# An encoder layer whose turned inputs come from the host, with a new opening

## The chip, the cores and the metric

The kernel runs on one core of a Trainium2 chip. The metric is the device time of one execution in microseconds (us), the median of several runs. Five engines work beside each other, each through its own instructions in a fixed order: TensorE (PE, matmuls and transposes; PEld is its loading of weights), VectorE (DVE), ScalarE (ACT), GpSimd (POOL) and SyncE (SP), which here issues nearly all DMA transfers. Across engines, semaphores hold an instruction back until what it reads is there and what it overwrites has been read.

## The reference

One layer over 2048 tokens of 1024 features, all in 32-bit floats:

```python
u = _rms_norm(h, norm_mix_g[l])
proj = u @ w_in[l]                                   # 1024 x 3600
hy = _short_conv_centred(proj[..., :HY_COLS], ...)   # 1536 columns
spec = _hyena_filter_spectrum(L, ...)                # from the weights alone
y_hy = _group_rms_norm(_hyena(hy, spec, hy_skip[l]), ...)
qk = jax.nn.silu(_short_conv_centred(proj[..., HY_COLS:off], ...))
y_ml = _group_rms_norm(_mlstm_bidirectional(qk, v, o, gates), ...)
h = h + concat(y_hy, y_ml) @ w_out[l]
h = h + _cross_attention(_rms_norm(h), _rms_norm(mem), xa_wq, xa_wk, xa_wv, xa_wo)
h = h + squared_relu(_rms_norm(h) @ ff_w1) @ ff_w2
out = _rms_norm(h, final_norm_g)
```

`_rms_norm(x, g)` is x / sqrt(mean(x*x over the 1024 features) + 1e-6) * g. The Hyena part convolves by FFT twice, gating after each; `mem` has 256 tokens.

## The kernel before, in words

A matmul contracts over the partition axis, so activations are needed with features on partitions ("turned") while `x` lies in memory with tokens as rows. Precision comes from splitting each 32-bit operand into a rounded high part and the remainder (`split`, L299: a copy on ACT, then a subtraction on DVE) and summing three products (`mm3`, lines 295 to 297).

**Opening and projection.** Half of x (1024 tokens) at a time lies turned, normalised and split in `xh` and `xl`. `prep` (L425) makes it tile by tile of 128 tokens: load rows (L401), square and sum on ACT (L409), a reciprocal root in eleven small DVE instructions (`rsqrt`, L144), scaling (L414), eight PE transposes of 128x128 (L420), a split into `xh` and `xl`. It is run for the first half, then the second, the first again, and for `mem`; `pop` advances it by a tile between matmul groups. `sweep` (L512) takes 256 columns of w_in at a time and runs four groups (two token blocks of 512 by two column blocks of 128) of 24 matmuls each, then the width-3 convolution, transposes of its result (`sweep_out`, L576) and stores; `natural` (L605) does the v, o and gate columns in 272- or 256-column matmuls.

**Filters and Hyena.** `filters` (L158) makes the filter spectrum: a small network (L208, L212), windows (L253, L238), writes to a scratch tensor `fs`, then 32 blocks that read it back, multiply (L284) and write `hd`. `hyena` (L638) runs two orders, each with a first transform (L720), 16 blocks that read `zs` and `hd` and write `zg` (L734, L702), and a last one (L753). `weave` takes steps of two generators in a fixed ratio: filters beside the first 1024 columns of w_in for both halves, Hyena beside the rest. All tensors between stages go through memory, so that a stage's reads wait for the writes before it.

**Later stages.** `memproj` (L458) projects mem and folds Wq and Wo into it; Wq is needed turned and `turned` (L331) does that with four PE transposes (L341) for each of 16 loads. `attention` (L1061) goes over four chunks of 512 tokens; its `residual` (L1131) loads rows of x, transposes them on PE (`turn`, L1106) and copies them into `acc`. Then comes the MLP.

A planner orders every engine's instructions before the run: program order is its input, but it moves instructions past each other where data allow. `keep_in_program_order` holds an instruction to its written place on its engine. A load from SP that must wait for its buffer holds all loads and stores behind it on SP.

```python
            p.prep_x(0, True)
            p.pop(4)
            s = chain(p.sweep(range(4), 0, True, lambda: p.prep_x(1)), p.sweep(range(4), 1, False))
            next(s)
            next(s)
            weave(p.filters(), s, 230, 200)
```

Of the kernel before, what the change touches and what calls it, by code (L numbers as in the profile page):

```python
# [19 lines left out]
D = 1024  # L20
# [77 lines left out]
class Prog:  # L98
    def __init__(self, ctx, tc, a):
        self.tc, self.nc, self.a = tc, tc.nc, a  # L100
        nc = self.nc
        self.ctx = ctx
        self.dr = ctx.enter_context(tc.tile_pool(name="dr", bufs=1, space=DRAM))
        self.s = {}
        cp = self.cp = ctx.enter_context(tc.tile_pool(name="cp", bufs=1))
        ident = cp.tile([128, 128], F32, name="ident")
        nc.gpsimd.memset(ident, 1.0)
        nc.gpsimd.affine_select(ident, ident, pattern=[[-1, 128]], compare_op=ALU.is_equal, fill=0.0,
                                base=0, channel_multiplier=1)
# [7 lines left out]
        self.prepq = None  # L117
        self.rbp = cp.tile([128, 16], F32, name="rbp")
        self.ps = ctx.enter_context(tc.tile_pool(name="ps", bufs=1, space=PSUM))
# [38 lines left out]
    def filters(self):  # L158
# [3 lines left out]
        with tc.tile_pool(name="f_sb", bufs=1, side="right") as sb:  # L162
# [56 lines left out]
            def windows(j2):  # L219
                if j2 == 8:  # L220
                    return None
                w = ta(), ta()
                for r in range(2):
                    nc.sync.dma_start(out=w[r], in_=wv[r, :, 2 * j2:2 * j2 + 2])
                return w
# [39 lines left out]
            def blocks(o, i):  # L265
                p, k = divmod(2 * i, 16)
                dm = sb.tile([128, 2, 128], F32, tag="dm", name="dm", bufs=3)
                nc.sync.dma_start(out=dm, in_=a["c_dm"][:, 2 * i:2 * i + 2])
# [30 lines left out]
    def split(self, hi, lo, src):  # L299
        self.nc.scalar.copy(hi, src)  # L300
        self.nc.vector.tensor_tensor(lo, src, hi.bitcast(F32), ALU.subtract)  # L301
# [10 lines left out]
    def weights(self, pool, w, n, kc=4, bufs=2, nbufs=2):  # L312
# [12 lines left out]
        for k0 in range(0, kt, kc):  # L325
            nat = pool.tile([128, kc, n], F32, tag="wn", name="wn", bufs=nbufs)
            nc.sync.dma_start(out=nat, in_=w[128 * k0:128 * (k0 + kc), :].rearrange("(k p) c -> p k c", p=128))
            self.split(hi[:, k0:k0 + kc], lo[:, k0:k0 + kc], nat)
        return hi, lo

    def turned(self, pool, w):  # L331
        nc = self.nc
        hi = pool.tile([128, 2, 1024], F32R, tag="wh", name="wh", bufs=2)
        lo = pool.tile([128, 2, 1024], F32R, tag="wl", name="wl", bufs=2)
        for i in range(4):
            nat = pool.tile([128, 2, 256], F32, tag="wn", name="wn", bufs=3)
            nc.sync.dma_start(out=nat, in_=w[256 * i:256 * i + 256, :].rearrange("(k p) c -> p k c", p=128))
            pt = self.mm()
            for m in range(2):
                for k in range(2):  # L340
                    nc.tensor.transpose(pt[:, 256 * m + 128 * k:256 * m + 128 * k + 128],  # L341
                                        nat[:, k, 128 * m:128 * m + 128], self.ident)
            ds = slice(256 * i, 256 * i + 256)
            self.split(hi[:, :, ds], lo[:, :, ds], pt.rearrange("p (m c) -> p m c", m=2))
        return hi, lo

    def stream(self, pool, items, **kw):
        nxt = None
        for i in range(len(items) + 1):
            cur = nxt  # L350
            if i < len(items):
                w, n = items[i]
                nxt = self.turned(pool, w) if n is None else self.weights(pool, w, n, **kw)
            if cur is not None:
                yield cur
# [3 lines left out]
    def inproj_open(self, es):  # L359
# [9 lines left out]
        self.g_mix = self.bcast(sb, a["norm_mix_g"], D, "g_mix")  # L369
        self.turned_to = lambda h: (self.xh[:, 4 * h:4 * h + 4], self.xl[:, 4 * h:4 * h + 4])  # L370
# [8 lines left out]
        nc.gpsimd.dma_start(out=self.cb[:, 12:20], in_=a["ml_conv_b"].rearrange("o (k p) -> p (o k)", p=128))  # L379
        self.gb = sb.tile([128, 16], F32, name="gb")  # L380
# [7 lines left out]
        second = [(a["xa_wq"][0][:, h], None) for h in hs] + [(a["xa_wo"][0][h, :], 1024) for h in hs]  # L388
# [4 lines left out]
        self.wst = self.stream(sb, items, kc=2, nbufs=3)  # L393

    def prep_load(self, src, first, i):
        sb = self.isb
        if first and i % 3:
            xn = sb.tile([128, 1042], F32, tag=("P", "cv")[i % 3 - 1], name="xn", bufs=2)[:, 0:D]
        else:
            xn = sb.tile([128, D], F32, tag="xn", name="xn", bufs=2)  # L400
        self.nc.sync.dma_start(out=xn, in_=src)  # L401
        return xn

    def prep_norm(self, xn, gain):
        nc, sb = self.nc, self.isb
        ss = sb.tile([128, 2], F32, tag="ss", name="ss", bufs=2)
        for h in range(2):
            junk = sb.tile([128, 512], F32, tag="st", name="junk", bufs=3)
            nc.scalar.activation(junk, xn[:, 512 * h:512 * h + 512], AF.Square, accum_out=ss[:, h:h + 1])  # L409
        ms = sb.tile([128, 1], F32, tag="ms", name="ms", bufs=2)  # L410
        nc.vector.tensor_tensor(ms, ss[:, 0:1], ss[:, 1:2], ALU.add)
        nc.vector.tensor_scalar(ms, ms, 1.0 / D, EPS, ALU.mult, ALU.add)
        rv = self.rsqrt(sb, ms, "xr")
        nc.vector.scalar_tensor_tensor(xn, xn, rv, gain, ALU.mult, ALU.mult)  # L414

    def prep_turn(self, xn, t):
        for h in range(2):
            p = self.mm().rearrange("p (k t) -> p k t", k=4)
            for k in range(4):
                self.nc.tensor.transpose(p[:, k], xn[:, 512 * h + 128 * k:512 * h + 128 * k + 128], self.ident)  # L420
            hi, lo = self.turned_to(h)
            ts = slice(128 * t, 128 * t + 128)
            self.split(hi[:, :, ts], lo[:, :, ts], p)

    def prep(self, src, gain, first=False):  # L425
        n = src.shape[0] // 128
        ahead = 5 if first else 1
        q = []
        for i in range(n + ahead):
            if i < n:  # L430
                xn = self.prep_load(src[128 * i:128 * i + 128, :], first, i)
                q.append(xn)
            if i >= ahead:
                xn = q.pop(0)
                self.prep_norm(xn, gain)
                self.prep_turn(xn, i - ahead)
                yield
# [6 lines left out]
    def prep_x(self, hf, first=False):  # L444
        self.prepq = self.prep(self.a["x"][1024 * hf:1024 * hf + 1024, :], self.g_mix, first)

    def mem_open(self):
        self.g_mem = self.isb.tile([128, D], F32, tag="g_mix", name="gm", bufs=1)
        self.nc.gpsimd.dma_start(out=self.g_mem, in_=self.a["norm_mem_g"].broadcast_to([128, D]))

    def prep_mem(self):
        sb = self.isb
        gm = self.g_mem
        self.memt = [[sb.tile([128, 4, 256], F32R, tag=tag, name="mt", bufs=2) for tag in ("P", "cv")] for h in range(2)]
        self.turned_to = lambda h: self.memt[h]
        self.prepq = self.prep(self.a["mem"], gm)
# [55 lines left out]
    def sweep(self, cols, hf, first, after=None):  # L512
        nc, a, sb = self.nc, self.a, self.isb
        xh, xl, cw, cb, carry = self.xh, self.xl, self.cw, self.cb, self.carry
        for c2 in cols:
# [8 lines left out]
            for c in range(2):  # L524
                for m in range(2):
# [5 lines left out]
                    for k in range(8):  # L531
                        self.mm3(p, wh[:, k, ms], wl[:, k, ms], xh[:, k, cs], xl[:, k, cs], k == 0, k == 7)
                    if c == 0:
# [527 lines left out]
    def attention(self, es):  # L1061
# [65 lines left out]
        stats = None  # L1127
        for c in range(4):
            acc = T.tile([128, 8, 512], F32, tag="acc", name="acc")

            def residual(h):  # L1131
                q = [rows(a["x"], 512 * c + 128 * t, h) for t in range(2)]
                for t in range(4):
                    xn = q.pop(0)
                    if t < 2:
                        q.append(rows(a["x"], 512 * c + 128 * (t + 2), h))
                    self.copy(acc[:, 4 * h:4 * h + 4, 128 * t:128 * t + 128], turn(xn))
# [500 lines left out]
def program(p):  # L1638
    with ExitStack() as ms:
        with ExitStack() as es:  # L1640
            p.inproj_open(es)
            p.prep_x(0, True)
            p.pop(4)
            s = chain(p.sweep(range(4), 0, True, lambda: p.prep_x(1)), p.sweep(range(4), 1, False))
            next(s)
            next(s)
            weave(p.filters(), s, 230, 200)
            p.flush()
            with ExitStack() as hs:
                weave(p.hyena(hs),  # L1650
                      chain(p.sweep(range(4, 10), 1, True), p.natural(1, (3, 0, 1, 2), lambda: p.prep_x(0)),
                            p.sweep(range(4, 10), 0, False, p.mem_open), p.natural(0, (3,), p.prep_mem, 2)),
# [49 lines left out]
```

## Time and profile before

| | |
|---|---|
| median of 3 runs | 3389.35 us (3387.64 to 3394.67) |
| the profiled execution | 3382.57 us, of which span 3380.9 us |
| PE busy | 3200.3 us, 95% of the span |
| DVE, ACT, POOL busy | 2044.1, 1491.3, 1265.5 us |
| moved by DMA | 674.55 MB, 200 GB/s on average |
| mean granted PE clock | 0.979 of full |

The span is the profiled core's time from its first to its last instruction. In a row of groups stand the source line, engine, operation, tiles written and read, shapes and count, then the busy time in us and the mean time of one in ns, then the idle time of the engine just before them with what ended it. Records of pipelined instructions overlap, so that a count times the mean is more than the busy time. A 32-bit matmul stands in the trace as two records.

### The profile page before, as it was taken

To read this page: it belongs to the slowest core of one execution; us is meant where nothing else is said; L and a number is where in the kernel's file an instruction comes from. 1 tells how busy PE (TensorE), PEld (TensorE's weight loads), DVE (VectorE), ACT (ScalarE), POOL (GpSimd) and SP (SyncE) were. 2 spreads that over 40 slices of the span, in tenths; PEclk is the share of its full clock that TensorE was granted. 3 is DMA by queue.
4 is the path that set the end of the run, shared out by engine and by line. 5 is a ranking of instruction groups with operands and counts; after the bars stand their busy time and mean duration, and the time that the engine had idled before them with its cause. 6 is when DMAs were issued, how large, how long until landed. Compare 5 with 4: busy or idle time off the path is not lost.

```text
span 3380.9 us, 46860 instructions
## 1 busy us (share of the span) xinstructions
PE 3200.3 (95%) x15671; PEld 2563.6 (76%) x15671; DVE 2044.1 (60%) x3711; ACT 1491.3 (44%) x2884; POOL 1265.5 (37%) x894
## 2 busy tenths in 40 slices
PE   6999999999999889799999999999999999999997
PEld 5656666677666778688887997888788887888876
DVE  7584324524646755777766554755855577555695
ACT  4344435523454235445444444555655543333335
POOL 2131001200222214534424013876766564434482
PEclk9999999999999999999999999999999999999998
DMA  5356889996999478857557445765654475444434
GB/s 165 116 206 204 278 294 253 283 337 230 242 242 285 154 240 272 270 152 230 182 162 252 147 132 163 226 204 176 209 165 159 146 241 174 128 140 134 134 94 159
DMA packets 480749, 674.55 MB, mean 200 GB/s; under 512 B 41738, under 2 KB 256848, under 8 KB 479484
## 3 DMA queue, kind: packets, MB, share of 16 engines
q1 hardware_dynamic: 478904, 668.70, 62.9%
q0 software_dynamic: 1600, 2.86, 0.4%
q8 instruction: 124, 2.03, 0.3%
q14 instruction: 117, 0.96, 0.1%
q10 hardware_dynamic: 4, 0.00, 0.0%
HBM read 452.23 MB, written 219.18 MB: 199 GB/s over the span
## 4 chain that ended last, share of the span: by engine, by line
PE 55%; DMA 10%; DVE 8%; issue 3%; ACT 2%; POOL 1%; SPq 0%; DVEq 0%; ACTq 0%; POOLq 0%
PE mm L297 11%; PE mm L295 11%; PE mm L296 11%; PE hy L297 5%; PE hy L295 5%; PE hy L296 5%; DVE wl L301 1%; DVE bl L1292 1%; DMA wr<-xs 1%; PE hy L753 1%; DMA rw<-rows 1%; PE hy L720 1%; DMA a<-hd 1%; DMA xn<-in_x_dram 1%; PE hy L1106 1%
## 5 line engine op out<-in xcount | busy, mean ns | idle before, releaser
L301 DVE TENSOR_TENSOR wl<-wn,wh 128x512 fp32r<-128x512 f32 (+1 forms) x352 | 276.0, 816 | 143.4 <-ACT wh L300 143.0
L1292 DVE TENSOR_TENSOR bl<-wr,bh 128x512 fp32r<-128x512 f32 x213 | 236.9, 1118 | 135.5 <-ACT bh L1291 133.3
L1291 ACT CAST ah<-w 128x512 fp32r<-128x512 f32 x284 | 176.2, 622 | 298.6 <-PE hy L296 154.2
L300 ACT CAST wh<-wn 128x512 fp32r<-128x512 f32 (+1 forms) x352 | 202.1, 617 | 216.0 <-PE mm L296 79.0
L295 PE MATMUL mm<-xh,wh 128*128 128x512 f32 x640 | 275.9, 432 | 8.7 <-ACT P L542 7.6
L739 POOL TENSOR_TENSOR b<-b,a 128x512 f32<-128x512 f32 x64 | 88.9, 1389 | 494.4 <-ACT b L737 207.4
L296 PE MATMUL mm<-xl,wh 128*128 128x512 f32 x640 | 266.0, 416 | 0.0
L297 PE MATMUL mm<-xh,wl 128*128 128x512 f32 x640 | 263.5, 412 | 0.2 <-DVE wl L301 0.2
L1292 DVE TENSOR_TENSOR al<-w,ah 128x512 fp32r<-128x512 f32 x236 | 225.6, 957 | 58.9 <-ACT ah L1291 58.9
L1291 ACT CAST bh<-wr 128x512 fp32r<-128x512 f32 x232 | 143.3, 621 | 245.8 <-PE mm L297 177.8
L297 PE MATMUL mm<-bh,al 128*128 128x512 f32 x576 | 224.4, 392 | 7.9 <-DVE al L1292 5.3
L295 PE MATMUL mm<-bh,ah 128*128 128x512 f32 x576 | 226.1, 393 | 0.4 <-DVE u L1417 0.3
L296 PE MATMUL mm<-bl,ah 128*128 128x512 f32 x576 | 224.9, 390 | 0.0
L295 PE MATMUL mm<-act,wh 128*128 128x512 f32 x512 | 201.6, 398 | 5.4 <-ACT wh L300 5.4
L296 PE MATMUL mm<-act,wh 128*128 128x512 f32 x512 | 203.4, 398 | 0.0
L297 PE MATMUL mm<-act,wl 128*128 128x512 f32 x512 | 201.5, 397 | 0.0
L1149 POOL TENSOR_TENSOR ssum<-ssum,sq 128x512 f32<-128x512 f32 x56 | 80.4, 1436 | 270.1 <-ACT sq L1148 267.3
L295 PE MATMUL hy<-bh,ah 128*128 128x512 f32 x448 | 175.2, 391 | 0.0
L296 PE MATMUL hy<-bl,ah 128*128 128x512 f32 x448 | 174.6, 390 | 0.0
L297 PE MATMUL hy<-bh,al 128*128 128x512 f32 x448 | 174.6, 390 | 0.0
L295 PEld LDWEIGHTS mm<-xh,wh 128*128 128x128 f32 x640 | 121.8, 190 | 55.5 <-issue 17.4
L295 PE MATMUL hy<-xh,ah 128*128 128x512 f32 x384 | 152.6, 398 | 9.1 <-ACT ah L1291 8.3
(379 smaller groups left out, 9046.3 us busy)
## 6 DMA issues: line engine op xcount, KB each, us to landing
wr<-hc SPq DMA_DIRECT2D x224, 256.0 KB
w<-in_ff_w_dram SPq DMA_DIRECT2D x176, 256.0 KB
a<-hd SPq DMA_DIRECT2D x128, 256.0 KB
hc<-t SPq DMA_DIRECT2D x128, 256.0 KB
wn<-in_w_in_dram SPq DMA_DIRECT2D x104, 256.0 KB
hc<-q SPq DMA_DIRECT2D x96, 256.0 KB
fs<-a SPq DMA_DIRECT2D x32, 512.0 KB
a<-fs SPq DMA_DIRECT2D x32, 512.0 KB
```

The costliest lines, as they stand in the source:

```text
L295: mm(ps, lh, rh, start=start, stop=False)
L296: mm(ps, lh, rl, start=False, stop=False)
L297: mm(ps, ll, rh, start=False, stop=stop)
L300: self.nc.scalar.copy(hi, src)
L301: self.nc.vector.tensor_tensor(lo, src, hi.bitcast(F32), ALU.subtract)
L720: nc.tensor.matmul(pp, f1[:, p], z[:, jj], start=True, stop=True)
L739: nc.gpsimd.tensor_tensor(xt, xt, hi[:, m], ALU.mult)
L753: nc.tensor.matmul(pp, e2[:, p], r[p][:, jj], start=p == 0, stop=p == 1)
L1106: nc.tensor.transpose(pt[:, 128 * k:128 * k + 128], yn[:, 128 * k:128 * k + 128], self.ident)
L1149: nc.gpsimd.tensor_tensor(ssum, ssum, sq, ALU.add)
L1291: self.nc.scalar.copy(hi, src)
L1292: eng.tensor_tensor(lo, src, hi.bitcast(F32), ALU.subtract)
```

## The change

The host gives three more arrays: x, mem and Wq transposed.

- In place of `prep`, `x_chunk` loads turned x by blocks of two 128-feature rows by 512 tokens. The scale of each token now lies along the free axis: it is spread over all partitions by a matmul of a matrix of ones with a diagonal matrix (`diagonal`, `spread`), and one DVE instruction applies it together with the gain.
- For the second half and for mem, the sums of squares come from natural rows, loaded once more early (`row_stats`). For the first half they come from the turned tiles: ACT squares, then 32 matmuls of one column for each block of 512 tokens (`add_up`).
- The opening, `x_first`, takes its buffers from an own pool `x_sb` on the side where `filters` later has its pool. It normalises tokens 0 to 511 as eight feature rows that the first matmuls follow, and hangs tokens 512 to 1023 into the first group of the sweep (`mid`). The program lets three steps of the sweep go ahead of the filters in place of two. Several instructions are kept in program order, some loads of windows and of `dm` among them.
- `turned` is gone; Wq is loaded like Wo. `residual` in the attention is one DMA of 1 MB straight into `acc`, which is now one tile for all four chunks.

```diff
-                    self.copy(acc[:, 4 * h:4 * h + 4, 128 * t:128 * t + 128], turn(xn))
+                src = a["x_t"].rearrange("(k p) t -> p k t", p=128)[:, 4 * h:4 * h + 4, 512 * c:512 * c + 512]
+                nc.sync.dma_start(out=acc[:, 4 * h:4 * h + 4], in_=src)
...
-        second = [(a["xa_wq"][0][:, h], None) for h in hs] + [(a["xa_wo"][0][h, :], 1024) for h in hs]
+        second = [(a["xa_wq_t"][h, :], 1024) for h in hs] + [(a["xa_wo"][0][h, :], 1024) for h in hs]
...
+    def diagonal(self, cols):
+        dg = self.isb.tile([128, 512], F32, tag="rb", name="dg", bufs=2)[:, 0:128 * cols.shape[1]]
+        for t in range(cols.shape[1]):
+            self.nc.vector.tensor_scalar(dg[:, 128 * t:128 * t + 128], self.ident, cols[:, t:t + 1], None, ALU.mult)
+        return dg
+
+    def spread(self, dg, pin=False):
...
+        d = self.nc.tensor.matmul(p[:, 0:n], self.ones, dg, start=True, stop=True)
...
+        self.nc.scalar.copy(rb[:, 0:n], p[:, 0:n])
+        return rb[:, 0:n]
...
+    def scaled(self, x, k0, gain, rb, hi, lo):
+        for k in range(x.shape[1]):
+            self.gained(x[:, k], gain[:, k0 + k:k0 + k + 1], rb)
+        self.split(hi, lo, x)
...
+    def x_chunk(self, c):
+        rb = self.spread(self.diagonal(self.rx[:, 4 * c:4 * c + 4]))
+        xs = [self.x_load(c, 0)]
+        for j in range(4):
+            if j < 3:
+                xs.append(self.x_load(c, j + 1))
+            to = slice(2 * j, 2 * j + 2), slice(512 * (c % 2), 512 * (c % 2) + 512)
+            self.scaled(xs.pop(0), 2 * j, self.g_mix, rb, *(t[(slice(None),) + to] for t in (self.xh, self.xl)))
+            yield
+
+    def x_first(self, own):
...
+        def add_up(ps, sq, k):
+            for t in range(4):
+                pin(nc.tensor.matmul(ps[t][:, 0:1], sq[:, 128 * t:128 * t + 128], self.ones[:, 0:1],
+                                     start=k == 0, stop=k == 7))
...
+        rb = self.spread(scale_of(0, ps))
+        sq = own.tile([128, 8, 512], F32, name="sq1")
+        write(x0, c0, rb, lambda k: square(sq[:, k], x1[k]))
+        yield
+        ps = [self.hy() for t in range(4)]
+        for k in range(8):
+            add_up(ps, sq[:, k], k)
+        dg = scale_of(1, ps)
+
+        def rest():
+            write(x1, c1, self.spread(dg, True))
+            w1 = self.weights(sb, *self.items[1], kc=2, nbufs=3, pin=True)
+            self.wst = self.stream(sb, self.items[2:], w1, kc=2, nbufs=3)
+        self.mid = rest
...
-            p.prep_x(0, True)
-            p.pop(4)
             s = chain(p.sweep(range(4), 0, True, lambda: p.prep_x(1)), p.sweep(range(4), 1, False))
-            next(s)
-            next(s)
+            with p.tc.tile_pool(name="x_sb", bufs=1, side="right") as own:
+                p.prepq = p.x_first(own)
+                p.pop()
+                next(s)
+                next(s)
+                next(s)
             weave(p.filters(), s, 230, 200)
```

More of the change, by code (lines that the diff above doesn't have):

```diff
@@ L117, in __init__ @@
         self.prepq = None
+        self.mid = None
         self.rbp = cp.tile([128, 16], F32, name="rbp")
@@ L310, in bcast, with weights @@
         return t
-    def weights(self, pool, w, n, kc=4, bufs=2, nbufs=2):
+    def weights(self, pool, w, n, kc=4, bufs=2, nbufs=2, pin=False):
         nc = self.nc
@@ L327, in weights, with stream @@
             nc.sync.dma_start(out=nat, in_=w[128 * k0:128 * (k0 + kc), :].rearrange("(k p) c -> p k c", p=128))
-            self.split(hi[:, k0:k0 + kc], lo[:, k0:k0 + kc], nat)
+            self.split(hi[:, k0:k0 + kc], lo[:, k0:k0 + kc], nat, pin)
         return hi, lo
[L331 to L349, printed above, removed]
-            cur = nxt
[L351 to L355, printed above, removed]
+    def stream(self, pool, items, cur, **kw):
+        for w, n in items:
+            nxt = self.weights(pool, w, n, **kw)
+            yield cur
+            cur = nxt
+        yield cur
     NAT_AT = (0, 2, 4)
@@ L416, in prep_turn @@
[L416 to L437, printed above, removed]
+        self.items = items
@@ L442, in pop, with prep_x, load, halves @@
                 self.prepq = None
[L444 to L449, printed above, removed]
+    def prep_x(self, hf):
+        self.prepq = chain(self.x_chunk(2 * hf), self.x_chunk(2 * hf + 1))
     def prep_mem(self):
         sb = self.isb
-        gm = self.g_mem
         self.memt = [[sb.tile([128, 4, 256], F32R, tag=tag, name="mt", bufs=2) for tag in ("P", "cv")] for h in range(2)]
-        self.turned_to = lambda h: self.memt[h]
-        self.prepq = self.prep(self.a["mem"], gm)
+        def load(h):
+            t = sb.tile([128, D], F32, tag="xn", name="xt", bufs=2).rearrange("p (k t) -> p k t", k=4)
+            self.nc.sync.dma_start(out=t, in_=self.a["mem_t"].rearrange("(k p) t -> p k t", p=128)[:, 4 * h:4 * h + 4])
+            return t
+        def halves():
+            xs = [load(h) for h in range(2)]
+            rb = self.spread(self.diagonal(self.rm))
+            for h in range(2):
+                self.scaled(xs[h], 4 * h, self.g_mem, rb, *self.memt[h])
+                yield
+        self.prepq = halves()
     def memproj(self):
```

134 lines of the change are left out of this document (102 added, 32 removed).

## The prediction

> **What bounds the kernel now.** I read the page's first two parts, then the idle reasons of PE, then the kernel by stages, because the change touches some stages and only shifts others.
>
> ```profile
> PE 3200.3 (95%) x15671; PEld 2563.6 (76%) x15671; DVE 2044.1 (60%) x3711; ACT 1491.3 (44%) x2884; POOL 1265.5 (37%) x894
> PE   6999999999999889799999999999999999999997
> DMA  5356889996999478857557445765654475444434
> ```
>
> PE is busy 95% of the span, so an instruction taken from PE is worth its time, if nothing else then becomes the limit. The third line warns where: in slices 7 to 13 (of 84.5 us) the DMA engines stand at 8 or 9 too. Next, the span cut where filter blocks (L284), first-order Hyena blocks (L734), its last transform (L753) and the second order begin and end. Columns: stretch, length, busy time and count of PE, PEld, DVE, ACT, POOL, then PE clock, DMA share, GB/s.
>
> ```profile
> 0.00:313.00 313.00, 284.64 (x1064) 182.66 (x1065) 219.98 (x496) 129.63 (x247) 76.23 (x63) 0.99 0.51 164
> 313.00:459.00 146.00, 144.07 (x570) 98.49 (x568) 36.03 (x53) 64.27 (x110) 0.00 (x0) 1.00 0.87 289
> 459.00:531.70 72.70, 71.43 (x282) 48.58 (x281) 27.88 (x43) 25.29 (x43) 0.59 (x1) 1.00 0.77 257
> 531.70:711.60 179.90, 167.74 (x704) 118.44 (x702) 86.65 (x135) 98.54 (x162) 43.77 (x32) 0.98 1.01 273
> 711.60:842.80 131.20, 126.98 (x732) 95.63 (x732) 48.71 (x114) 35.94 (x83) 0.00 (x0) 1.00 0.79 289
> 842.80:1058.50 215.70, 202.05 (x788) 141.49 (x789) 114.53 (x202) 112.94 (x187) 45.70 (x33) 0.97 0.94 248
> 1058.50:1124.20 65.70, 53.94 (x218) 35.69 (x216) 58.42 (x137) 15.95 (x28) 27.24 (x17) 0.92 0.79 273
> 1124.20:3380.90 2256.70, 2149.40 (x11325) 1842.62 (x11323) 1451.88 (x2534) 1008.72 (x2028) 1071.95 (x748) 0.98 0.56 179
> ```
>
> Their lengths add up to the span. In the fourth row the DMA share is 1.01: there the queue is full, and 167.74 us of PE work only just covers it. The chain of waits shows the same near the end of that stage: it runs through transfers, not PE.
>
> ```profile
> 682.44 9.30 DMA zg<-a
> 691.75 7.48 DMA a<-hd
> ```
>
> **The change, part by part.** The prices, from groups by shape on PE and from DVE and ACT:
>
> ```profile
> L295 PE MATMUL mm<-xh,wh 128*128 128x512 f32 x640 | 275.9, 432 | 8.7 <-ACT P L542 7.6 <-ACT xh L300 1.0
> L720 PE MATMUL hy<-a,f 128*128 128x512 f32 x128 | 60.9, 593 | 1.3 <-DMA a<-hy 1.3
> L1221 PE MATMUL hy<-ones,ssum 128*128 128x1 f32 x32 | 3.8, 240 | 0.0
> L1106 PE MATMUL hy<-ident,wn 128*128 128x128 f32 x256 | 40.5, 301 | 18.9 <-DMA wn<-in_x_dram 8.7 <-DMA wn<-yh 7.0 <-DMA wn<-ym 2.5
> L420 PE MATMUL mm<-ident,xn 128*128 128x128 f32 x208 | 33.5, 306 | 32.0 <-DVE xr_t L153 16.3 <-DVE hr_t L154 6.9 <-DVE xr_t L154 4.5
> L341 PE MATMUL mm<-ident,wn 128*128 128x128 f32 x64 | 11.3, 322 | 12.9 <-DMA wn<-in_xa_wq_dram 8.0 <-ACT ab L809 2.8 <-DVE pad L823 1.4
> 48.04 0.39 PE L295 MATMUL mm<-xh,wh 128*128 128x512 f32 x1
> 48.27 0.39 PE L296 MATMUL mm<-xl,wh 128*128 128x512 f32 x1
> 52.38 1.47 PE L420 MATMUL mm<-ident,xn 128*128 128x128 f32 x12
> L153 DVE TENSOR_TENSOR xr_t<-xr_y 128x1 f32<-128x1 f32 x78 | 17.2, 226 | 0.9
> L301 DVE TENSOR_TENSOR xl<-mm,xh 128x512 fp32r<-128x512 f32 x48 | 31.8, 682 | 3.6 <-ACT xh L300 3.5
> L300 ACT CAST xh<-mm 128x512 fp32r<-128x512 f32 x48 | 26.4, 589 | 14.5 <-PE mm L420 14.4
> ```
>
> Records overlap, so I price a matmul by the step to the next start. A 512-column product takes 0.23 us (48.04 to 48.27), a 256- or 272-column one half, 0.12. A full 32-bit 512-column one has two records, 60.9/64 = 0.95 us. A one-column one (two records of L1221) takes 3.8/16 = 0.24. A transpose takes 1.47/12, less the tail of the last, 0.115.
>
> *Removed:* 208 + 64 + 128 (half of L1106's 256) = 400 transposes, 46 us. *Added:* 64 one-column matmuls (15 us) and 7 spreads of 0.95 (7 us). Net, PE loses 24 us. DVE loses most of its reciprocal roots, ACT nothing much; neither sets the end. DMA gains 5 MB (natural rows for sums, 1 MB of mem), loaded before 100 us, where the queue has room; the head of SP then waits for buffers of the rows, with w_in pieces behind it, which costs PE about 1 us, taken into the 31 us below.
>
> *Opening.* Before, the first product starts at 30.72, a pause ends at 44.29, and by 60 us PE has done 45 products that read `xh`, two of each three, so 67 of the 96 in the first four groups:
>
> ```profile
> 4.67 0.63 ACT L409 ACTIVATE junk<-xn 128x512 f32<-128x512 f32 x1 [2.57 <-DMA xn<-in_x_dram]
> 30.72 1.42 PE L295 MATMUL mm<-xh,wh 128*128 128x512 f32 x1
> 44.29 0.65 PE L295 MATMUL mm<-xh,wh 128*128 128x512 f32 x1 [2.77 <-ACT P L542]
> 44.74 0.63 PE L296 MATMUL mm<-xl,wh 128*128 128x512 f32 x1
> 0.00:30.00 30.00, 0.00 (x0) 0.00 (x0) 4.12 (x6) 4.04 (x7) 0.00 (x0) 1.00 0.97 256
> 30.00:60.00 30.00, 17.61 (x45) 9.72 (x45) 6.67 (x10) 4.95 (x9) 0.00 (x0) 0.94 0.47 150
> ```
>
> The other 29 need 6.7 us and a filter matmul 1: four groups at 68. After: 2.1 MB of x and 1 MB of weights at 256 GB/s, from about 2.5 us (the first 0.5 MB is there at 4.67), are in at 15. ACT's order puts the last squares behind the weight copies: 17; four sums, cold, 19; some twenty small DVE steps of 0.226, 23.4; the spread, cold, 25; copy, scaling, cast, 27. Then 48 products, 11.1 us plus 1.7 for the cold start, to 39.8 (a scaling and a subtraction on DVE, 1.4 us, for each six products: even). Then nothing but the second block's sums, 32 x 0.24 = 7.6, to 47.4, the small steps again, 51.3, spread and copies, 54.2, and 48 products, cold: four groups at 67. That is level, within -4 and +8. The gain is spent on two chains in a row where PE waits.
>
> After the 2.77 us pause, products start 0.45 us apart, twice as slow, so I charge 1.7 us for each such pause. The Trainium skill, "TensorE: Matmul & The Clock Gate", Part 1 ("The HAM clock gate"), says that the clock halves only after an idle window of about 3.4 us; were my second pause, split by the spread, too short for that, the sum would be 1.7 us less.
>
> *What the opening displaces.* The filters' pool waits for `x_sb`, so filters start some 50 us later, and the built order on PE moves with that: before the first L284 stand 869 of the 512-column products (520 before), and fewer are left to run beside blocks and Hyena. Pricing the built order by stage, against the rows above:
> - to the first block: 64 x 0.24 + 140 x 0.95 + 869 x 0.232 + 256 x 0.115 = 379 us of PE, plus 31 of pauses (27 less the sums in it, 5 between the blocks of tokens, 4 cold, 2 later): 410, against 313.
> - blocks: 63 x 0.95 + 264 x 0.232 + 64 x 0.115 = 128, with small waits 132, against 146. Same bytes at a share of 0.87/132x146 = 0.96: it fits.
> - to the first Hyena block: 78, against 72.7.
> - first order: 64 x 0.95 + 16 x 0.232 + 644 x 0.12 + 16 x 0.115 = 143 of PE. The built order of SP has 48.7 MB here (51.0 before); the queue was full, so 179.9 x 48.7/51.0 = 172. PE waits 29 us, about 17 more than now.
> - between: 127, against 131.2.
> - second order: 169 of PE, 50.9 MB against 53.8; at a full queue 215.7 x 0.94 x 50.9/53.8 = 192, and PE alone with its present 14 us of waits 183; I take 190.
> - its end: 55 of PE plus the present 12 less 2: 65.
> - the rest: 200 transposes (23 us) fewer, and 116 x 0.116 + 96 x 0.123 = 25 us of products moved ahead of it. The waits L1106 <- x (8.7) and L341 <- Wq (8.0) also go, since PE no longer touches those tiles: 2256.7 - 48 - 16.7 = 2192.
>
> Sum: 410 + 132 + 78 + 172 + 127 + 190 + 65 + 2192 = 3366, 15 us under the span of 3380.9. The profiled execution took 3382.57, so 3368; the median of the runs is 6.8 above that execution, so **3374**, 0.4% faster.
>
> The residual DMA into `acc` waits for the store of the previous chunk, and SP with it, the next weights queued behind. Its first reader comes five groups later (5 x 24 x 0.23 = 28 us), against a store and a load of 1 MB at 179 GB/s, 6 us each; I cost it at nothing, at 4 x 6 = 24 if that cover is gone.
>
> **Rivals.**
> 1. *The queue keeps up* and Hyena stays bound by PE: first order 143 + 12, second 169 + 14, so 24 us less: 3350. For it, a stretch that moved far more at the same share:
>
> ```profile
> 740.00:760.00 20.00, 20.00 (x112) 14.73 (x111) 5.40 (x9) 2.95 (x7) 0.00 (x0) 1.00 1.04 411
> ```
>
> At 411 GB/s 48.7 MB need 118 us. Against it, other transfers ran there; the block stage itself gave 273 at a full share. The Trainium skill, "DMA: Bandwidth & Descriptors", Specifications, gives about 358 GB/s of memory for a core, 136 us for these bytes, by which this rival would hold; the 273 of the row decides against it.
>
> 2. *Slower: the queue-bound stages keep their lengths.* Reads of `zs` wait for writes in order, and SP issues them in turn, so blocks 146, first order 180, second 216 as now, however little PE has to do: 48 us more than my sum, 3422. It decides from 15 us on: when the three together take over 509 us instead of my 494. For it, the second order ran 13.65 us over its PE work at a share under 1, so it is not bytes alone.
>
> 3. *The waits only change names*: memory projection and attention wait for the weights' split or for `y`, nothing of 16.7 us goes: 3391, no change.
>
> **How the numbers follow.** Chances: the forecast (3360 to 3382) 0.38, queue keeps up 0.14, slower 0.33, waits renamed 0.15. The range takes in the first rival less 12 us for openings and waits that go better, and the second: 3338 to 3422; the likeliest case's own is 3360 to 3382. A change under 0.2% is about what measurement can't tell: faster 0.52, same 0.15, slower 0.33.
>
> **What would show it.** In the profile after: first product near 27, a pause of PE near 47 to 54, four groups by 67; the first filter block near 410; the first order about 172 long at a DMA share of 1, with PE idle near 30 in it; no L341 in memory projection and PE busy there above the present 163.75 of 185.8 us:
>
> ```profile
> 1124.20:1310.00 185.80, 163.75 (x1282) 158.83 (x1281) 97.04 (x281) 67.91 (x129) 34.92 (x31) 0.94 0.67 204
> ```
>
>  A first order of 155 or of 180 tells rivals 1 and 2 apart. I am wrong if the planner's new order stalls a later stage (mLSTM, MLP), which this sum takes as unchanged.

## The result, and the profile after

The changed kernel takes **3410.77 us** (median of 7 runs, 3405.30 to 3427.84) against 3390.64 (7 runs) of the kernel before: a ratio of 1.0069, 95% interval 1.0052 to 1.0087. It is slower by 0.7%; forecast were 3374 us and 0.4% faster. The profiled execution spans 3409.1 us, 43 more than the 3366 of the forecast's sum.

The first part of its page, and the span cut at the same places as in the prediction (stretch, length, busy time and count of PE, PEld, DVE, ACT, POOL, PE clock, DMA share, GB/s):

```profile
PE 3216.0 (94%) x15413; PEld 2557.3 (75%) x15413; DVE 2022.0 (59%) x3469; ACT 1466.2 (43%) x2803; POOL 1271.1 (37%) x894
```

```profile
0.00:439.40 439.40, 406.85 (x1534) 276.19 (x1535) 245.93 (x445) 165.04 (x285) 77.06 (x64) 0.97 0.46 144
439.40:562.60 123.20, 123.01 (x457) 80.80 (x455) 26.71 (x41) 61.93 (x102) 0.00 (x0) 1.00 0.96 338
562.60:637.60 75.00, 75.00 (x277) 50.59 (x276) 28.88 (x45) 28.72 (x45) 0.57 (x1) 1.00 0.78 274
637.60:812.40 174.80, 150.94 (x805) 113.47 (x804) 68.07 (x103) 79.97 (x146) 43.09 (x32) 0.93 1.00 266
812.40:932.90 120.50, 120.50 (x484) 80.18 (x483) 57.11 (x84) 35.55 (x56) 0.00 (x0) 1.00 0.89 326
932.90:1122.10 189.20, 172.38 (x675) 118.52 (x674) 98.18 (x147) 103.61 (x167) 44.95 (x32) 0.96 1.00 261
1122.10:1184.10 62.00, 57.00 (x278) 40.00 (x276) 53.39 (x108) 8.46 (x17) 25.17 (x15) 0.94 0.81 281
1184.10:3409.10 2225.00, 2110.28 (x10912) 1797.57 (x10910) 1443.72 (x2501) 982.89 (x1989) 1080.31 (x750) 0.97 0.57 180
```

Four hundred transposes are gone, and PE is nevertheless busy 15.7 us longer than the 3200.3 before. Against the forecast, stage by stage: to the first filter block 439 in place of 410 (29 more); the six stretches after it 745 in place of 764 (19 less); the rest 2225 in place of 2192 (33 more). 29 - 19 + 33 = 43. So the error has two places, and the queue-bound middle, which I had feared most, is not one of them.

**The first place** begins in the opening. PE's timeline (start, length, line, tiles, shape, count, idle before), rows of the sums (L465), the spreads (L422) and the first products of each token block (L300), then ACT's first cast of the weights:

```profile
5.69 8.69 PE L465 MATMUL hy<-ones,sq 128*128 128x1 f32 x40 [5.69 <-ACT sq L460]
19.27 5.28 PE L465 MATMUL hy<-ones,sq 128*128 128x1 f32 x24 [4.89 <-ACT sq L460]
28.17 2.07 PE L422 MATMUL mm<-dg,ones 128*128 128x512 f32 x2 [3.62 <-DVE dg L416]
32.36 1.22 PE L300 MATMUL mm<-xh,wh 128*128 128x512 f32 x2 [2.11 <-ACT xh L481]
44.65 9.38 PE L465 MATMUL hy<-ones,sq 128*128 128x1 f32 x64
57.57 2.08 PE L422 MATMUL mm<-dg,ones 128*128 128x512 f32 x2 [2.48 <-DVE dg L416]
61.76 1.22 PE L300 MATMUL mm<-xh,wh 128*128 128x512 f32 x2 [2.11 <-ACT xh L481]
```

```profile
17.26 0.62 ACT L305 CAST wh<-w 128x512 fp32r<-128x512 f32 x1 [6.12 <-DMA w<-in_w_in_dram]
```

The first product comes at 32.4 (forecast 27), the second block's at 61.8 (forecast 54.2), and the four groups end at 76 (forecast 67): 9 of the 29 us. The shape of the opening was right; its loads and sums were too cheap. The weights came at 17.3, where the forecast had all of it in at 15 with 256 GB/s: from 5 to 17 us the DMA moved 160 GB/s at a share of 1.22. Then 12 of the first block's matmuls of sums were left (24 records, 19.27 to 24.55), where the forecast had four and their end at 19. The sums took 14.0 and 9.4 us in the two blocks, where 7.7 was priced for each.

The other 20 lie between 76 and 439. There stand the 64 filter matmuls of L256 and L257 (L253, L254 before): a forward and a backward one of 64 rows each, on opposite halves of the partitions. Two excerpts of PE's timeline:

```profile
203.64 1.45 PE L241 MATMUL hy<-b,f 128*128 128x512 f32 x3
205.02 0.80 PE L256 MATMUL hy<-w,hid 64*128 64x512 f32 x1
205.02 0.80 PE L257 MATMUL hy<-w,hid 64*128 64x512 f32 x1
205.66 0.59 PE L256 MATMUL hy<-w,hid 64*128 64x512 f32 x1
205.66 0.59 PE L257 MATMUL hy<-w,hid 64*128 64x512 f32 x1
206.18 0.50 PE L300 MATMUL mm<-xh,wh 128*128 128x512 f32 x1
...
211.59 1.23 PE L256 MATMUL hy<-w,hid 64*128 64x512 f32 x2
212.75 0.50 PE L301 MATMUL mm<-xl,wh 128*128 128x512 f32 x1
213.08 0.40 PE L302 MATMUL mm<-xh,wl 128*128 128x512 f32 x1
...
213.55 0.40 PE L301 MATMUL mm<-xl,wh 128*128 128x512 f32 x1
213.88 1.23 PE L257 MATMUL hy<-w,hid 64*128 64x512 f32 x2
```

At 205.02 the two stand next to each other and run side by side: both are done after 1.16 us (205.02 to 206.18). At 211.59 three products follow the forward one, and the backward one comes alone at 213.88: each now takes 1.16 us, and the product ahead of each visit and the one behind it step 0.33 us to the next in place of 0.23 (213.55 to 213.88, 212.75 to 213.08). The Trainium skill, "TensorE: Matmul & The Clock Gate", Part 3 (packing small matmuls), says that matmuls on different row groups of the array run concurrently; the two equal starts agree.

What the group costs in all is shown by the busy time of the instructions that touch tile `hid`, in a window that holds them all; first the kernel before, then the changed one:

```profile
0.00:460.00 460.00, 56.23 (x128) 24.54 (x128) 2.53 (x4) 1.00 0.62 204
```

```profile
0.00:460.00 460.00, 68.47 (x128) 28.75 (x128) 2.52 (x4) 0.97 0.48 152
```

The same 128 records (64 matmuls) take 12.2 us more. They form 64 pairs of a forward and a backward record. From their starts, 31 pairs ran side by side before and 16 do now, in 55 visits of PE to the group in place of 43 (the expectations below give the number of pairs too, "of 128 records"). A group's busy time takes in records that overlap their neighbours; by the step to the next start, as the prediction prices, the group takes 53.4 us before and 64.6 now. I had priced it 64 x 0.95 = 61; to the 64.6 come 55 visits at 0.2 us each, 11 us. That makes 15 of the 20 us. From the end of the opening PE also idles 11.7 us, where the forecast put 2:

```profile
76.00:439.40 363.40, 351.75 (x1304) 230.42 (x1303) 213.19 (x360) 135.76 (x232) 61.65 (x39) 0.99 0.46 149
```

Against these 25 us stands some 7, since the 76 other full 32-bit matmuls took 0.85 us each and not 0.95 (below).

**The second place** is the rest of the kernel, cut into memory projection with mLSTM, attention, and MLP. Before, then after:

```profile
1124.50:1412.50 288.00, 249.37 (x1830) 235.93 (x1830) 179.41 (x473) 118.04 (x283) 95.59 (x75) 0.92 0.75 232
1412.50:2085.90 673.40, 650.58 (x3984) 579.29 (x3983) 440.85 (x1017) 305.74 (x731) 209.27 (x150) 0.98 0.56 177
2085.90:3380.90 1295.00, 1249.16 (x5514) 1027.40 (x5512) 831.32 (x1047) 584.93 (x1014) 767.09 (x523) 0.98 0.52 168
```

```profile
1184.10:1445.70 261.60, 215.28 (x1570) 201.94 (x1569) 176.64 (x466) 102.81 (x263) 98.72 (x77) 0.92 0.82 252
1445.70:2108.90 663.20, 636.60 (x3832) 565.69 (x3831) 440.37 (x990) 295.59 (x713) 212.36 (x150) 0.98 0.56 176
2108.90:3409.10 1300.20, 1258.41 (x5514) 1029.94 (x5512) 826.71 (x1047) 584.49 (x1014) 769.22 (x523) 0.98 0.53 168
```

PE's work fell as priced: 34 us in the first (forecast 7 + 1 + 25), 14 in attention (15). The idle time didn't: it rose from 38.6 to 46.3 and from 22.8 to 26.6, where 16.7 less was forecast. PE's waits in the first stretch (waited for: us in total, times, longest), before and after:

```profile
PE mm L341 <- DMA wn<-in_xa_wq_dram: 8.0, 5, 2.5
PE hy L1106 <- DMA wn<-yh: 7.0, 2, 6.7
PE mm L296 <- DVE wl L301: 3.7, 3, 1.9
```

```profile
PE mm L300 <- ACT wh L305: 12.5, 6, 7.3
PE hy L1199 <- DVE ht L1101: 10.6, 1, 10.6
```

and ACT's at its start:

```profile
ACT wh L305 <- DMA wn<-in_xa_wq_t_dram: 17.5, 6, 9.0
```

PE's wait for Wq is gone, and in its place PE waits for ACT's split of the weights, which itself waits 17.5 us for Wq; PE also waits for mLSTM's own chain (`ht`).

### The profile page after: what moved, and what is told of

Read it like the earlier page. It is cut to its first block, busy times and chain, and to the rows that moved or that the text cites. A ratio compares the mean times of both kernels' runs of the same rounds, so it can differ in the third digit from the quotient of the medians.

```text
span 3409.1 us, 45966 instructions
## 1 busy us (share of the span) xinstructions
PE 3216.0 (94%) x15413; PEld 2557.3 (75%) x15413; DVE 2022.0 (59%) x3469; ACT 1466.2 (43%) x2803; POOL 1271.1 (37%) x894
## 4 chain that ended last, share of the span: by engine, by line
PE 70%; DMA 13%; DVE 9%; issue 3%; ACT 2%; POOL 1%; SPq 1%; ACTq 0%; DVEq 0%; POOLq 0%
PE mm L302 14%; PE mm L300 14%; PE mm L301 14%; PE hy L302 5%; PE hy L300 5%; PE hy L301 5%; DMA a<-hd 3%; DVE wl L305 2%; PE hy L241 2%; PE hy L813 2%; PE hy L289 1%; PE hy L256 1%; DMA zg<-a 1%; PE hy L846 1%; PE mm L669 1%
## 5 line engine op out<-in xcount | busy, mean ns | idle before, releaser
L305 DVE TENSOR_TENSOR wl<-wn,wh 128x512 fp32r<-128x512 f32 (+1 forms) x364 | 286.0, 820 | 117.3 <-ACT wh L305 107.6
L300 PE MATMUL mm<-xh,wh 128*128 128x512 f32 x640 | 274.4, 436 | 7.1 <-ACT xh L481 4.2
L301 PE MATMUL mm<-xl,wh 128*128 128x512 f32 x640 | 275.7, 432 | 0.7 <-DVE xl L305 0.7
L302 PE MATMUL mm<-xh,wl 128*128 128x512 f32 x640 | 272.1, 426 | 0.0
L300 PE MATMUL mm<-bh,ah 128*128 128x512 f32 x576 | 227.4, 395 | 0.0
L300 PE MATMUL mm<-act,wh 128*128 128x512 f32 x512 | 202.1, 398 | 6.8 <-ACT wh L305 6.8
L300 PE MATMUL hy<-bh,ah 128*128 128x512 f32 x448 | 175.2, 391 | 0.0
L300 PEld LDWEIGHTS mm<-xh,wh 128*128 128x128 f32 x640 | 122.0, 191 | 62.8 <-issue 26.9
L265 POOL TENSOR_TENSOR b<-b 128x512 f32<-128x512 f32 x32 | 58.3, 1822 | 286.6 <-DVE b L260 146.5
```

Of the source, the lines that this page charges most:

```text
L265: nc.gpsimd.tensor_tensor(e[1], f, b, ALU.subtract)
L300: mm(ps, lh, rh, start=start, stop=False)
L301: mm(ps, lh, rl, start=False, stop=False)
L302: mm(ps, ll, rh, start=False, stop=stop)
L305: both = (self.nc.scalar.copy(hi, src), self.nc.vector.tensor_tensor(lo, src, hi.bitcast(F32), ALU.subtract))
```

## The experiments

My theory once the result was known: (a) the opening's sums and the filter pairs cost what the transposes gave, (b) in the rest the waits only changed names. The rivals: the residual DMA or the turned Wq does the harm; the half clock does it; or the displaced filters do. All ratios are against the kernel before.

**One part alone, twice.** First the residual:

```diff
-                    self.copy(acc[:, 4 * h:4 * h + 4, 128 * t:128 * t + 128], turn(xn))
+                src = a["x_t"].rearrange("(k p) t -> p k t", p=128)[:, 4 * h:4 * h + 4, 512 * c:512 * c + 512]
+                nc.sync.dma_start(out=acc[:, 4 * h:4 * h + 4], in_=src)
```

> The kernel before with one part of the change: the residual goes by DMA from turned x into one accumulator tile; opening, projection and Wq as before. It takes 128 transposes from PE in attention, 128 x 0.115 = 15 us, and the wait of L1106 for rows of x (8.7 us). If the residual is harmless and its wait only moves to another name: 15 us less than before, some 3376. If the wait goes as well, as the prediction had it: 24 less, 3367. If the residual is what costs (the transfer of 1 MB waits on SP for the store of the chunk ahead, the weights behind it): not below before, 3390 or more, with attention longer and PE waiting there for weights.

3381.83 us, ratio 0.9973 (0.9958 to 0.9987). By the ratio it gains 9 us; PE is busy 15.6 less, as priced. Attention alone in this kernel:

```profile
1424.10:2079.50 655.40, 632.73 (x3832) 562.86 (x3832) 440.54 (x987) 295.60 (x713) 212.57 (x149) 0.98 0.57 178
```

It is 18 us shorter with 17.9 less of PE work; PE idles 22.7 us there, 22.8 before. The residual is no harm and its transfer is covered, but the 8.7 us of waiting for rows of x went to other names. That is the first case expected, at 9 of its 15 us. In this execution the stages ahead of the rest, which the edit doesn't touch, took 12 us more (they end at 1136.2, not 1124.5); I didn't find out why.

```diff
-        second = [(a["xa_wq"][0][:, h], None) for h in hs] + [(a["xa_wo"][0][h, :], 1024) for h in hs]
+        second = [(a["xa_wq_t"][h, :], 1024) for h in hs] + [(a["xa_wo"][0][h, :], 1024) for h in hs]
```

> The kernel before with one other part alone: Wq comes turned from the host and is loaded like Wo. It takes 64 transposes from PE in the projection of mem, 7 us, and the wait of L341 for Wq (8.0 us). If the wait is only renamed (the split of the weights on ACT and DVE is what PE then waits for): 7 less than before or nothing, 3384 to 3391. If the wait goes too: 15 less, 3376. If this part costs: above 3391, with a wait for the weights' split in the projection of mem larger than 8 us.

3382.03 us, 0.9987 (0.9976 to 0.9999). PE is busy 4.2 us less (7 priced) and the gain is about as much. Its waits in the first stretch of the rest:

```profile
PE mm L295 <- ACT wh L300: 6.9, 6, 1.9
PE mm L296 <- DVE wl L301: 4.9, 3, 3.8
```

Before, PE waited 8.0 us for Wq at L341 and 3.7 for the split of weights at L296, together 11.7; now it waits 6.9 and 4.9 for the split, 11.8. That the wait is only renamed is shown by the part alone.

**The opening taken back** in the changed kernel (natural rows, transposes, two steps ahead):

```diff
-            with p.tc.tile_pool(name="x_sb", bufs=1, side="right") as own:
-                p.prepq = p.x_first(own)
-                p.pop()
-                next(s)
-                next(s)
-                next(s)
+            p.prepq = p.x_first()
+            p.pop(4)
...
+            next(s)
+            next(s)
```

> The changed kernel with its opening taken back: the first half of x is normalised from natural rows with transposes on PE, filters start as early as before; the later loads of turned x, mem, Wq and the residual stay changed. If the opening and what it displaces are the loss: 128 + 64 + 64 + 16 transposes of the 400 stay out, 31 us, less 4 spreads (4 us), so 27 us under before, 3364, and the first filter block near 313 again, the rest (after the Hyena part) 20 to 30 us under before's 2256.7. If the loss sits in the residual, Wq or the later loads: within 10 us of the changed kernel, 3400 or more, with a long rest and a normal opening.

3381.75 us, 0.9980 (0.9966 to 0.9995): 7 us under before, not 27. The residual and Wq are cleared, but most of the gain is missing. The first filter block came at 366.2, not near 313, a miss; the rest took 2225.0 us, 32 under before's (20 to 30 expected) and just as long as in the changed kernel. The group on `hid` is even dearer here, with 6 pairs side by side:

```profile
0.00:460.00 460.00, 74.58 (x128) 31.27 (x128) 2.50 (x4) 0.98 0.60 197
```

**The second block's sums from natural rows:**

```diff
-        ps = [self.hy() for t in range(4)]
-        for k in range(8):
-            add_up(ps, sq[:, k], k)
-        dg = scale_of(1, ps)
+        nc.vector.tensor_tensor(ss[:, 0], ss[:, 0], ss[:, 1], ALU.add)
+        self.inv_rms(self.rx[:, 4:8], ss[:, 0])
+        dg = self.diagonal(self.rx[:, 4:8])
```

> The changed kernel, with the sums of squares of its second token block taken from natural rows (four more loads of 0.5 MB, ACT sums them) in place of 32 one-column matmuls. The pause from 44.65 to 61.76 then shrinks: the second block's first product at some 47 in place of 61.8. If the opening's time reaches the end: 10 to 15 us less than the changed kernel, 3396 to 3401. If what is saved there is lost again because filters and the Hyena part set the pace: 3406 to 3411, with the later stages at the changed kernel's lengths. If the loads harm the opening (the queue was full until 30): the first product later than 32.4 and no gain.

3394.47 us, 1.0022 (1.0008 to 1.0036): 16 us under the changed kernel.

```profile
46.45 1.07 PE L422 MATMUL mm<-dg,ones 128*128 128x512 f32 x2
51.06 1.22 PE L300 MATMUL mm<-xh,wh 128*128 128x512 f32 x2 [3.54 <-ACT xh L481]
```

The second block's products start at 51.1 (47 expected), 10.7 earlier, and the first filter block at 429.4 in place of 439.4. These 10 us reach the end: the opening is on the path. Where the other 6 come from isn't shown.

**The filter pairs held together**, by an ordering edge alone:

```diff
-                        nc.tensor.matmul(pf, hid[0:64, j::16], w3[0:64, o], start=True, stop=True)
+                        mf = nc.tensor.matmul(pf, hid[0:64, j::16], w3[0:64, o], start=True, stop=True)
+                        while freed:
+                            tc.add_manual_dep(mf.ins, freed.pop().ins.name, no_sync, reason="pair")
```

(`freed` holds the last readers of the four buffers.) In the changed kernel:

> The changed kernel, with one thing added: an ordering edge holds the forward filter matmul (L256) back until the buffers of both are free, so that it and the backward one (L257) stand next to each other on PE, 32 visits in place of 55. In the trace the two lie on different halves of the rows and run side by side where they stand together (one pair 1.16 us, one alone 1.16 us too); 31 of their 128 records did so before the change and 16 after it, and the group went from 53.4 to 64.6 us. If the change lost time by separating them: the group falls to some 38 us and the first filter block comes 25 to 30 us earlier, near 412; the end 20 to 30 us earlier than the changed kernel, 3381 to 3391. If the pairs are nothing on the path (the extra waiting for buffers takes it back): 3405 to 3411.

3384.06 us, 0.9987 (0.9975 to 0.9999): 27 us under the changed kernel, and no longer slower than the kernel before as it stands. All but 2 of the 64 pairs now run side by side.

```profile
0.00:460.00 460.00, 40.74 (x128) 17.06 (x128) 2.52 (x4) 0.97 0.51 161
```

The group fell by 27.7 us, and the end by as much. The first filter block came only 5.7 us earlier (433.7), not 27, since the planner put 114 more records ahead of it (1648 in place of 1534); the gain appears as less work later. With the row sums as well:

> The changed kernel with both repairs: sums of the second token block from natural rows, and the filter pairs side by side. If the two losses are independent and on the path: 16 us (measured for the first) and 20 to 30 more, 3365 to 3375, below before. If they share the same slack: 3390 to 3395, no better than the first repair alone.

3373.98 us, 0.9955 (0.9942 to 0.9968). The two repairs together take 37 of the 43 us that they take alone.

In the kernel before, with residual and Wq:

> The kernel before, old opening and all, with the residual by DMA, Wq turned by the host, and the filter pairs held together. The two measured alone took 9 and 5 us, so 14 together; the pairs fall from 53.4 to some 38 us, 15 more, and 2 us of switching: 3390 - 31 = 3359 if all three add up. If the pairs do nothing here: 3374. If residual and Wq gain the same time twice: 3366 or more.

**3359.19 us**, 0.9920 (0.9902 to 0.9937): the expected 3359, and better than both kernels. The number is in part luck, since it counted 17 us for the pairs, which alone give 12, and the ratio itself means 27 us and not 31. The pairs alone in the kernel before:

> The kernel before with the filter pairs held together and nothing else. Its group takes 53.4 us in 43 visits; with 50 or more of 128 records side by side it should take 40 to 46 in 32, so 8 to 13 us less and 2 for switching: 3375 to 3380. If the pairs gain is nothing without the other parts: 3390. If it is larger than the group (the filters end earlier and the queue-bound stages start earlier): 3370 or less.

3376.85 us, 0.9963 (0.9946 to 0.9979); its group on `hid`:

```profile
0.00:460.00 460.00, 44.31 (x128) 19.83 (x128) 2.53 (x4) 0.99 0.63 206
```

11.9 us less than 56.23, and 12 us less at the end. The ratios add up: 0.27 + 0.13 + 0.37 = 0.77% alone, 0.80% together.

So 12 of the 27 us that held pairs give the changed kernel are to be had in the kernel before as well, and the fair comparison holds the pairs in both. Then the changed kernel is still some 7 us slower (3384.06 against 3376.85), and level only with its sums repaired too (3373.98). The pairs that the change parted thus cost it some 15 us.

**Work under the pause**, 18 matmuls that nothing reads:

```diff
+                pin(nc.tensor.matmul(warm, w0[0][:, 0, 0:128], self.xh[:, 0, c0], start=True, stop=True))
...
+            idle_work(1)
+        idle_work(10)
```

> The changed kernel with 18 512-column matmuls that nothing reads, placed among and after the second block's one-column sums, which only adds work to PE in the opening. In the changed kernel the clock stood at half from 49.7 to 66.7 us, beginning while PE issued one-column matmuls without a pause. If one-column matmuls do not keep the clock up and that costs: half clock there only in 3.4 us pieces, products after 61.8 at full speed, and 3 to 6 us less at the end, 3405 to 3408. If the clock there costs nothing, because the scale's chain sets the time: 3411 or above.

3412.31 us, 1.0075 (1.0060 to 1.0089), no gain. Two of the groups of eight sum records, early and late:

```profile
43.31 0.95 PE L465 MATMUL hy<-ones,sq 128*128 128x1 f32 x8
...
51.30 1.70 PE L465 MATMUL hy<-ones,sq 128*128 128x1 f32 x8
```

The granted clock fell among the sums all the same (0.61 on average from 44 to 54 us), with one large matmul after every eight of their records, and they went at half pace. That the half clock is the loss is not borne out; that it is no part of it isn't shown either, since the added work took time itself.

**The old opening again, its flaw mended and its pairs held.** In the run with the old opening the gain row came late; loaded first:

```diff
+        self.g_row = self.bcast(sb, a["norm_mix_g"], D, "g_row")
         self.g_mix = self.column(a["norm_mix_g"], 8, "g_mix")
```

> The run with the old opening again, with one flaw of it mended: its gain row came over POOL's queue only at 23 us, so that the first transposes started at 25.0 in place of some 10. It is now the first load of that queue. If the opening's time reaches the end: 10 to 15 us less than that run's 3382, 3367 to 3372. If the filters set the pace there whatever the opening does: 3380.

3393.37 us, 1.0011 (0.9996 to 1.0026). A miss: transposes started at 10.4 as meant, yet the kernel is 12 us slower than with the flaw. Its first filter block came at 374.8 (366.2) with 39 more records of PE ahead of it (1171 in place of 1132), and PE is busy 7.0 us more over the same 15345 records; I can't say why. With the pairs held:

> The same, with the filter pairs held side by side. With the old opening in the changed kernel only 6 of the 128 filter records ran side by side and the group took 70.4 us in 60 visits; held together it should take some 38 in 33. If the lost pairs are what kept the old opening from showing the transposes' gain (27 us expected, 7 measured): 33 us less for the group and 5 for switching, 3330 to 3345, below every kernel so far. If something else kept it: above 3355.

3361.11 us, 0.9910 (0.9892 to 0.9928): 32 us less, as much as expected from the group, but 3361 lies in the branch above 3355, since it starts from a slower kernel than was assumed. Two comparisons follow. With the later loads the same and the pairs held, the new opening with its sums repaired takes 3373.98 us (0.9955) and the old one 3361.11: the new opening costs 13 us more. Whether that is the filters that it still displaces or what is left of its two chains isn't shown. And the kernel before with pairs, residual and Wq is as fast (3359.19), so that turned loads of x and mem in the projection bring nothing that the end shows.

**Five raw weight buffers** on the best kernel:

```diff
-        self.wst = self.stream(sb, items, kc=2, nbufs=3)
+        self.wst = self.stream(sb, items, kc=2, nbufs=5)
```

> The kernel before with residual, Wq and held pairs, and five raw weight buffers in place of three, so that Wq's pieces can be asked for earlier. In the changed kernel the wait for Wq stayed, through ACT's split: ACT waited 17.5 us for its transfers at the start of the projection of mem, PE 12.5 for ACT. If it is the buffers that hold the loads back: those waits fall by half or more and the end comes 5 to 8 us earlier than with three buffers, 3351 to 3354. If the stretch is set by something else (the mLSTM's own chain beside it, or the queue): 3357 to 3361, with other waits in their place.

3361.46 us, 0.9918 (0.9892 to 0.9944), no gain. PE's wait for the split in the first stretch of the rest, with three buffers and with five:

```profile
PE mm L298 <- ACT wh L303: 12.8, 9, 3.5
```

```profile
PE mm L298 <- ACT wh L303: 3.9, 2, 3.7
```

So the buffers did hold the loads back, and the stretch fell from 280.6 to 269.0 us, as the first branch had it. But it starts 15.8 us later (1136.1 in place of 1120.3), the Hyena stages ahead of it being longer. The end is that of the second branch; whether the longer stages follow from the edit stays open.

## Why the prediction was wrong

Point by point, by its own steps:

- **Removed and added.** Right for most transposes: 128 alone took 15.6 us of PE's busy time (priced 15); 64 took 4.2 (7). Wrong for the sums: 23.4 us in place of 15. The first block's took 0.22 us a record (24 in 5.28), which is the pace of half clock in the run with work under the pause (8 in 1.70), not of full (8 in 0.95). The clock column doesn't show this part: it reads 1.00 from 20 to 36 us, where products too step 0.43 us at first.
- **Opening.** Called level within -4 and +8 against 68; it ended at 76, the outer end. The steps that failed are "are in at 15" with "four sums, cold, 19", which ended at 24.6, some 5.5 us late, and "32 x 0.24 = 7.6", which took 9.4. The repair of the second block by row sums shows that the opening counts at the end.
- **What the opening displaces.** The count was right: 128 + 280 + 869 + 256 = 1533 records to the first filter block forecast, 1534 found. The price was not. "140 x 0.95" took the mean of a 128-row matmul for 64 that run two at a time or alone, depending on their neighbours. I read the planner's new order for its counts, not for what stood next to what. This is the step that failed most: held together, the pairs give 27 us back in the changed kernel, 12 of which the kernel before could have as well.
- **Blocks, Hyena.** Better than forecast by 19 us. Part of it is the same 0.95, too dear for 128-row matmuls (three records of L241 in the quoted timeline go from 203.64 to 205.02, 0.1 of it for the switch, so 0.85 a matmul of two records). The first order came out as drawn: 174.8 us (172) at a share of 1.00 and 266 GB/s, PE idle 23.9 (29).
- **The rest.** PE's work fell as priced, the 16.7 us of waits didn't go, and in the stretch that lost the 25 us of products moved ahead PE's idle time rose by 7.7, so that it became only 26 us shorter for 34 us less work. "Also go" is the step that failed. Of the 33 us, 5 are in the MLP (below).
- **Residual at nothing.** Right: alone it is a gain.
- **Rivals.** The first (the queue keeps up) fell: the first order took 175, not 155. The second had the sign but not the cause: its three stages took 487 us, under its point of 509. That 3411 lies inside the stated range, which reaches up to this rival's 3422, is luck. The third had the mechanism of the rest right. What was named last, a new order by the planner that stalls something, is nearest to the main cause, only that nothing stalls: PE is busier.

What the change's gain was spent on is thus shown for the second block's sums (16 us, 10 with the pairs held) and for the parted pairs (27 us to be had by holding them, of which some 15 are the change's own); of the third item, waits, it is shown that Wq's was renamed. Why waits further on take the place of those removed, and why the old opening with its gain loaded early is slower, stays open.

## What to carry to other kernels

Where a planner orders the instructions, count not only how many move past a place but which neighbours part: here two matmuls on different halves of the rows took 1.16 us together if they touched and 1.16 us each if a third came between, and no total in the profile says so (busy time by tile does). Compare the repaired kernel with an equally repaired one before: part of what a repair gives is not the change's loss. A wait of PE for a transfer need not go when PE no longer touches the tile: for Wq it passed to the engine that took PE's place (11.7 us before, 11.8 after). And a sum over features by one-column matmuls isn't cheap: one took 0.95/4 = 0.24 us at full clock, as long as a product of 512 columns (0.23), and 1.70/4 = 0.43 at half.

## What the runs showed of the hardware that I had not expected

The clock fell while PE issued without a pause. PE in two stretches of the changed kernel's opening:

```profile
44.00:54.00 10.00, 10.00 (x69) 9.87 (x67) 0.47 (x3) 0.59 (x1) 0.00 (x0) 0.77 0.00 0
54.00:62.00 8.00, 3.41 (x6) 1.11 (x6) 4.68 (x20) 4.49 (x12) 0.00 (x0) 0.50 0.42 132
```

From 44 to 54 PE is busy throughout, nearly all of it with one-column matmuls, and the granted clock is 0.77 on average, then 0.50 up to 62. The Trainium skill, "TensorE: Matmul & The Clock Gate", Part 1, ties the halving to an idle window; here PE had no gap when the clock fell, but issued one-column matmuls. In the run with work under the pause it fell among such matmuls too.

In the MLP, which no edit touches, the changed kernel's products are slower by 1.4%; the same group before and after:

```profile
L295 PE MATMUL hy<-xh,ah 128*128 128x512 f32 x384 | 152.6, 398 | 9.1 <-ACT ah L1291 8.3 <-ACT xh L1315 0.8
```

```profile
L300 PE MATMUL hy<-xh,ah 128*128 128x512 f32 x384 | 154.8, 404 | 7.3 <-ACT ah L1380 6.5 <-ACT xh L1404 0.8
```

Every kernel with the new loads of turned x in the projection shows 1254 to 1260 us of PE there, the others 1249 to 1252, in one profiled execution each. The cause stays open.
